# A hybrid decoder layer on one core: earlier table load and TensorE run-up, vectors behind x, and a reordered end

## The chip, the cores and the metric

The kernel runs on one core of a Trainium2 chip. The metric is the device time of one launch in microseconds. The kernel before took 1624.99 us (median of three runs, 1622.81 to 1625.93).

Five engines appear in the profile. TensorE is shown as PE for the matmuls and PEld for the loads of their stationary operand. VectorE is DVE, ScalarE is ACT, GpSimd is POOL, and SyncE is SP. SP issues nearly all transfers. ACT issues a few on a queue of its own, between its own instructions. Each engine works through its instructions in the order in which they stand.

## The reference

One layer works on x of 256 positions by 2048 channels, in float32. In short:

```
h    = rmsnorm(x) * norm_mix_w
proj = h @ w_in            -> q, k, v, z, b, a, p_in, g_a, g_b
q, k, v = silu(causal convolution over 4 positions); q and k normalised per head
o    = gated delta rule over 16 heads, chunked (a triangular solve per chunk)
y_a  = rmsnorm(o) * silu(z)
y_b  = (trailing means of p_in over 2, 4, 8, 16 positions - p_in) @ pool_w * pool_scale
x    = x + (sigmoid(g_a) * y_a + sigmoid(g_b) * y_b) @ w_out
h    = rmsnorm(x) * norm_ffn_w
gate, up = split(h @ w_up)
x    = x + (gelu(convolution over 3 positions of gate) * up) @ w_down
out  = rmsnorm(x) * norm_final_w
```

## The kernel before

The 256 positions are two tiles `t` of 128. All weights are streamed once in tiles of 256 rows by 512 columns (512 KB). There are 530 such transfers, two of them in another shape for the columns of b and a. A float32 product is formed from three fast products. `whi` is the weight rounded to the fast format (ACT, L110), `wlo` is the rest (DVE, L117), and the activations are split in the same way into `xhi` (ACT, L236) and `xlo` (DVE, L237). The matmuls of one weight tile are then twelve: L147 (`xhi` by `whi`), L148 (`xlo` by `whi`) and L149 (`xhi` by `wlo`), for two row blocks and two `t`. (The up projection swaps the roles of weights and activations, L171 and L172.) The weights go through three pools: `raw` with four buffers, `whi` and `wlo` with three each. `begin(n)` starts the load and the split of the next weights, `weights()` hands out the next pair.

The order of the instructions of each engine is not the order of the code. A scheduler places them by a simulated time line and by priority, engine by engine. The compiled order of an engine is therefore looked up, not read from the code.

At the start, x arrives as four tiles of 512 columns by `t` (`x_0` to `x_3`, L216), with the weight loads in between (L108). PE turns each x tile by transposes (L232) into `psg`. ACT makes `xhi` from it, scaled by the norm's weights `nmw`, which come in as rows (`nmrows`, L212) and are transposed as well (L223). DVE then makes `xlo`. The first product, the first 512 columns of k, runs over eight weight tiles. The small vectors of the layer (`vrows`, `cqrows`, `cfrows`, `alb`, `dtb`, `gwb`, and `psb`, which is pool_scale repeated on 128 partitions, 256 KB) come on ACT's queue. The squares of x for the norm (L310) run on ACT. Their sum gives `rs1`, which is first needed where the first product is taken out of the accumulator (L431).

In the middle, groups of four heads run their delta rule on DVE, POOL and small matmuls beside the big products. The up projection and the down projection follow.

At the end, the down projection adds 22 weight row blocks into four column accumulators `c` for each `t`. `acc[0]` and `acc[1]` lie in `psg`, `acc[2]` and `acc[3]` in `psm`. The last row block is taken in the order of `t`. Then for each `t` the accumulator is added to x (DVE, L848), squared and summed (ACT, L850), the four sums are reduced and scaled (DVE, L852 and L853), and raised to the power -1/2 (POOL, L854). Columns 2 and 3 are multiplied by the norm's weights `nfin` ahead of that (DVE, L857) and by the row factor after it (ACT, L864). Columns 0 and 1 get both at once (DVE, L861). Eight transfers write the result (SP, L865).

Of the kernel before, what the change touches and what calls it, by code (L numbers as in the profile page):

```python
# [20 lines left out]
EPS = 1e-6  # L21
# [4 lines left out]
B0 = 32  # L26
NR = P // B0
AHEAD = 2
WAIT = 5


@with_exitstack
def kernel(
# [44 lines left out]
    srcs = []  # L78
# [15 lines left out]
    made = []  # L94
    taken = [0]

    def weights():

        begin(taken[0] + AHEAD + 1)
        taken[0] += 1  # L100
        return made[taken[0] - 1]

    def begin(n):
        while len(made) < min(len(srcs), n):
            src = srcs[len(made)]
# [4 lines left out]
            nc.scalar.copy(hi, raw)  # L110
            if shape[1] == 8:
                lo = None
                nc.vector.tensor_tensor(hi[:, :, 32:64], raw[:, :, 0:32], hi[:, :, 0:32].bitcast(F32),
                                        op=ALU.subtract)
            else:
                lo = wpool.tile(shape, F32R, tag="wlo", name=nm("wlo"))
                nc.vector.tensor_tensor(lo, raw, hi.bitcast(F32), op=ALU.subtract)  # L117
            made.append((hi, lo))

# [16 lines left out]
    def gemm_a(lh, ll, nk):  # L136

        ps = pm()
        for c in range(nk // 2):
            if c == 1:  # L140
                while later:
                    later.pop(0)()
            hi, lo = weights()
            for kk in range(2):
                k = 2 * c + kk
                for t in range(2):
                    mm(ps[:, t, :], lh(k, t), hi[:, kk, :], start=(k == 0), stop=False)  # L147
                    mm(ps[:, t, :], ll(k, t), hi[:, kk, :], start=False, stop=False)  # L148
                    mm(ps[:, t, :], lh(k, t), lo[:, kk, :], start=False, stop=(k == nk - 1))  # L149
                side()  # L150
        return ps
# [45 lines left out]
    ones = cpool.tile([P, P], F32, name="ones")  # L197
# [28 lines left out]
    xhi, xlo = xhl[:, :, 0, :], xhl[:, :, 1, :]  # L226
    for k2 in range(KD // 2):
        pt = pg([P, 2, S])
        for kk in range(2):
            k = 2 * k2 + kk  # L230
            for t in range(2):
                nc.tensor.transpose(pt[:, kk, t * P : (t + 1) * P], x0[k // 4][:, t, (k % 4) * P : (k % 4 + 1) * P],  # L232
                                    ident)
        for kk in range(2):
            k = 2 * k2 + kk
            nc.scalar.activation(xhi[:, k, :], pt[:, kk, :], AF.Copy, scale=nmw[:, k : k + 1])  # L236
            nc.vector.scalar_tensor_tensor(xlo[:, k, :], pt[:, kk, :], nmw[:, k : k + 1], xhi[:, k, :].bitcast(F32),  # L237
                                           op0=ALU.mult, op1=ALU.subtract)

# [5 lines left out]

    ps_k0 = gemm_a(xh, xl, KD)


    NV = 16 + KF
    V_FFN, V_CB = 0, 16  # L250
# [15 lines left out]
    pv = pg()  # L266
# [3 lines left out]
    pv = pg()  # L270
# [4 lines left out]
    pv = pg()  # L275
# [88 lines left out]
    for c in range(2):  # L364
        hi, lo = weights()
        for kk in range(8):
            k = 8 * c + kk
# [86 lines left out]
    def gdn(g, kq, vT, res):  # L454
# [84 lines left out]
        yield  # L539
        for _ in range(WAIT):  # L540
            yield
# [16 lines left out]
        for h in range(4):  # L558
# [110 lines left out]
    for g in range(4):  # L669
# [88 lines left out]
    fp = ctx.enter_context(tc.tile_pool(name="ffn", bufs=1))  # L758
    xt = fp.tile([P, 2, D], F32, name="xt")
# [4 lines left out]
    for c in range(4):  # L764
        ps = gemm_a(at(mhi), at(mlo), KD)
        xs = xt[:, :, c * 512 : (c + 1) * 512]
        nc.vector.tensor_tensor(xs, xs, ps, op=ALU.add)
        for t in range(2):
            jk = cpool.tile([P, 512], F32, tag="sqj", name=nm("sqj"))
            nc.scalar.activation(jk, xs[:, t, :], AF.Square, accum_out=ssq4[:, t, c : c + 1])  # L770
        for k2 in range(2):
            pt = pg([P, 2, S])
            for kk in range(2):
                k = 4 * c + 2 * k2 + kk
                for t in range(2):
                    nc.tensor.transpose(pt[:, kk, t * P : (t + 1) * P], xt[:, t, k * P : (k + 1) * P], ident)
            for kk in range(2):
                k = 4 * c + 2 * k2 + kk
# [3 lines left out]
                                               op0=ALU.mult, op1=ALU.subtract)  # L782
# [45 lines left out]
    def down_part(kp, c, t, hi, lo):  # L828
        for kk in range(2):
            k = 2 * kp + kk  # L830
            mm(acc[c][t], lh(k, t), hi[:, kk, :], start=(k == 0), stop=False)  # L831
            mm(acc[c][t], ll(k, t), hi[:, kk, :], start=False, stop=False)  # L832
            mm(acc[c][t], lh(k, t), lo[:, kk, :], start=False, stop=(k == KF - 1))  # L833
# [6 lines left out]
                down_part(kp, c, t, *w)  # L840
    ws = [weights() for c in range(3)]
    ssq5 = cpool.tile([P, 2, 4], F32, name="ssq5")
    for t in range(2):
        for c in range(1, 4):
            down_part(LAST, c, t, *ws[c - 1])
        for c in range(4):
            xs = xt[:, t, c * 512 : (c + 1) * 512]
            nc.vector.tensor_tensor(xs, xs, acc[c][t], op=ALU.add)  # L848
            jk = cpool.tile([P, 512], F32, tag="sqj", name=nm("sqj"))
            nc.scalar.activation(jk, xs, AF.Square, accum_out=ssq5[:, t, c : c + 1])  # L850
        rs = cpool.tile([P, 1], F32, name=nm("rs"))
        nc.vector.tensor_reduce(rs, ssq5[:, t, :], axis=mybir.AxisListType.X, op=ALU.add)  # L852
        nc.vector.tensor_scalar(rs, rs, 1.0 / D, EPS, op0=ALU.mult, op1=ALU.add)  # L853
        nc.gpsimd.tensor_tensor(rs, rs, epsx[:, 0:1], op=ALU.pow)  # L854
        for c in (2, 3):
            xs = xt[:, t, c * 512 : (c + 1) * 512]
            nc.vector.tensor_tensor(xs, xs, nfin[:, c * 512 : (c + 1) * 512], op=ALU.mult)  # L857
        for c in (0, 2, 1, 3):
            xs = xt[:, t, c * 512 : (c + 1) * 512]
            if c < 2:  # L860
                nc.vector.scalar_tensor_tensor(xs, xs, rs, nfin[:, c * 512 : (c + 1) * 512],  # L861
                                               op0=ALU.mult, op1=ALU.mult)
            else:
                nc.scalar.activation(xs, xs, AF.Copy, scale=rs)  # L864
            nc.sync.dma_start(out[0, t * P : (t + 1) * P, c * 512 : (c + 1) * 512], xs)  # L865


# [29 lines left out]
```

## Time and profile before

| | |
|---|---|
| median of three runs | 1624.99 us (1622.81 to 1625.93) |
| the profiled execution: time, span | 1624.68 us, 1623.0 us |
| PE busy | 1577.3 us, 97% of the span |
| DVE, ACT, POOL busy | 1090.8, 753.5, 165.3 us |
| read from memory | 287.07 MB, 179 GB/s over the span |
| first matmul of a weight tile | 9.26 us after the span's start |
| last matmul ends | 1612.5 us after the span's start |

The span runs from the first instruction to the last; the profiled execution took 1.7 us more than its span. Times in the profile are counted from the span's start. A row of the time line has the start, the duration, the engine, the line of the kernel, the operation, what it writes and reads, and in brackets the idle time of the engine ahead of it and what ended it. Neighbouring equal instructions are merged into one row with their count; successive instructions overlap a little, so the durations of a group's members add up to more than its step. Matmuls are pipelined: the step from one start to the next, not the duration, is what a matmul costs in a stream.

### The profile page before, as it was taken

The numbers are of one execution on the slowest core, as the hardware profiler recorded it, in microseconds if no ns is written. First come the engines' busy times: TensorE is split into PE (matmuls) and PEld (weight loads), VectorE is DVE, ScalarE is ACT, GpSimd is POOL, SyncE is SP. The second block draws the span as 40 slices with busy tenths as digits, with TensorE's granted clock in tenths as the row PEclk, the third lists the DMA queues.
The fourth block names the chain that finished last, engine by engine and source line by source line (L and its number), as shares of the span: only waits on it lengthen the run. The fifth ranks groups of instructions, "written<-read, shape, count | busy, mean of one in ns | idle before, by whom it ended". The sixth has DMA issues, their size and how long they took to land.

```text
span 1623.0 us, 21418 instructions
## 1 busy us (share of the span) xinstructions
PE 1577.3 (97%) x8084; PEld 1319.9 (81%) x8084; DVE 1090.8 (67%) x1612; ACT 753.5 (46%) x977; POOL 165.3 (10%) x176
## 2 busy tenths in 40 slices
PE   8998999989999999989999999999999999999997
PEld 6876888878887788867788888888888888888886
DVE  5878757786678857796555766666667676444445
ACT  6454445434455435443355544444444444433334
POOL 1022100221013300141000000000000000000000
PEclk9999999999999999999999999999999999999999
DMA  7654645555556655555365655655655556655553
GB/s 247 182 164 150 195 145 177 169 171 173 156 156 171 174 173 164 168 147 170 138 228 181 187 190 186 191 185 192 192 185 192 185 193 204 200 194 194 194 194 131
DMA packets 159790, 291.62 MB, mean 180 GB/s; under 512 B 17974, under 2 KB 21062, under 8 KB 159302
## 3 DMA queue, kind: packets, MB, share of 16 engines
q1 hardware_dynamic: 157792, 285.77, 56.7%
q10 hardware_dynamic: 1894, 4.48, 0.8%
q8 instruction: 63, 1.03, 0.2%
q14 instruction: 41, 0.34, 0.1%
HBM read 287.07 MB, written 3.15 MB: 179 GB/s over the span
## 4 chain that ended last, share of the span: by engine, by line
PE 85%; DVE 7%; DMA 3%; issue 2%; POOL 2%; SPq 0%; DVEq 0%; POOLq 0%; ACT 0%
PE psm L149 12%; PE psm L148 11%; PE psm L147 11%; PE psm L171 10%; PE psg L171 10%; PE psg L172 5%; PE psm L172 5%; DVE wlo L117 3%; PE psg L831 2%; PE psg L832 2%; PE psg L833 2%; PE psm L831 2%; PE psm L833 2%; PE psm L832 2%; DVE tb L549 2%
## 5 line engine op out<-in xcount | busy, mean ns | idle before, releaser
L117 DVE TENSOR_TENSOR wlo<-raw,whi 128x1024 fp32r<-128x1024 f32 x528 | 658.6, 1249 | 416.8 <-ACT whi L110 406.3
L110 ACT CAST whi<-raw 128x1024 fp32r<-128x1024 f32 x530 | 557.5, 1053 | 769.5 <-PE psm L148 353.1
L149 PE MATMUL psm<-wlo,xhl 128*128 128x512 f32 x896 | 358.0, 400 | 18.3 <-DVE wlo L117 18.2
L147 PE MATMUL psm<-whi,xhl 128*128 128x512 f32 x896 | 355.6, 397 | 1.4 <-ACT xhl L236 1.4
L148 PE MATMUL psm<-whi,xhl 128*128 128x512 f32 x896 | 355.1, 396 | 0.0
L171 PE MATMUL psm<-fhl,whi 128*128 128x512 f32 x704 | 245.9, 396 | 0.0
L171 PE MATMUL psg<-fhl,whi 128*128 128x512 f32 x704 | 237.8, 394 | 0.0
L149 PEld LDWEIGHTS psm<-wlo,xhl 128*128 128x128 f32 x896 | 170.6, 190 | 58.3 <-DVE wlo L117 23.7
L147 PEld LDWEIGHTS psm<-whi,xhl 128*128 128x128 f32 x896 | 170.9, 191 | 35.8 <-ACT xhl L236 1.8
L148 PEld LDWEIGHTS psm<-whi,xhl 128*128 128x128 f32 x896 | 170.5, 190 | 35.4
L172 PE MATMUL psm<-fhl,wlo 128*128 128x256 f32 x704 | 194.2, 279 | 0.0
L172 PE MATMUL psg<-fhl,wlo 128*128 128x256 f32 x704 | 178.6, 279 | 0.0
L171 PEld LDWEIGHTS psm<-fhl,whi 128*128 128x128 f32 x704 | 131.4, 188 | 30.4
L171 PEld LDWEIGHTS psg<-fhl,whi 128*128 128x128 f32 x704 | 129.2, 188 | 24.0
L172 PEld LDWEIGHTS psg<-fhl,wlo 128*128 128x128 f32 x704 | 132.5, 188 | 6.9
L172 PEld LDWEIGHTS psm<-fhl,wlo 128*128 128x128 f32 x704 | 132.5, 188 | 1.1
L806 POOL TENSOR_TENSOR y<-y,rb 128x1024 f32<-128x1024 f32 x11 | 27.3, 2485 | 457.6 <-ACT y L805 457.6
L831 PE MATMUL psg<-whi,hhi 128*128 128x512 f32 x176 | 68.6, 390 | 0.0
L832 PE MATMUL psg<-whi,hlo 128*128 128x512 f32 x176 | 68.5, 389 | 0.0
L831 PE MATMUL psm<-whi,hhi 128*128 128x512 f32 x176 | 68.5, 389 | 0.0
L832 PE MATMUL psm<-whi,hlo 128*128 128x512 f32 x176 | 68.5, 389 | 0.0
L833 PE MATMUL psm<-wlo,hhi 128*128 128x512 f32 x176 | 68.5, 389 | 0.0
(232 smaller groups left out, 1617.7 us busy)
## 6 DMA issues: line engine op xcount, KB each, us to landing
raw<-in_w_in_dram SPq DMA_DIRECT2D x226, 512.0 KB, 3.8
raw<-in_w_up_dram SPq DMA_DIRECT2D x176, 512.0 KB, 3.5
raw<-in_w_down_dram SPq DMA_DIRECT2D x88, 512.0 KB, 4.3
raw<-in_w_out_dram SPq DMA_DIRECT2D x32, 512.0 KB, 3.6
raw<-in_pool_w_dram SPq DMA_DIRECT2D x8, 512.0 KB, 4.1
x<-in_x_dram SPq DMA_DIRECT2D x4, 512.0 KB, 8.0
lb<-cdd SPq DMA_DIRECT2D x16, 128.0 KB, 2.8
xt<-in_x_dram ACTq DMA_DIRECT2D x1, 2048.0 KB, 9.9
```

Of the source, the lines that this page charges most:

```text
L110: nc.scalar.copy(hi, raw)
L117: nc.vector.tensor_tensor(lo, raw, hi.bitcast(F32), op=ALU.subtract)
L147: mm(ps[:, t, :], lh(k, t), hi[:, kk, :], start=(k == 0), stop=False)
L148: mm(ps[:, t, :], ll(k, t), hi[:, kk, :], start=False, stop=False)
L149: mm(ps[:, t, :], lh(k, t), lo[:, kk, :], start=False, stop=(k == nk - 1))
L171: mm(ps[f], hi[:, kk, fs], rhl(k), start=(k == 0), stop=False, skip_group_check=True)
L172: mm(ps[f][:, 1, :], lo[:, kk, fs], rhl(k)[:, 0, :], start=False, stop=(k == nk - 1), skip_group_check=True)
L549: nc.vector.tensor_tensor(tb[:, :, j + 1 :], tb[:, :, j + 1 :], tv, op=ALU.subtract)
L806: nc.gpsimd.tensor_tensor(y, y, rb2b, op=ALU.mult)
L831: mm(acc[c][t], lh(k, t), hi[:, kk, :], start=(k == 0), stop=False)
L832: mm(acc[c][t], ll(k, t), hi[:, kk, :], start=False, stop=False)
L833: mm(acc[c][t], lh(k, t), lo[:, kk, :], start=False, stop=(k == KF - 1))
```

## The change

At the start, one element is copied on ACT ahead of all other work there, which puts the load of the function table at that place. Eleven matmuls of a tile of ones with itself are put ahead of PE's other work; their result is not used. The first x tile comes in two halves of 256 columns, with the first weight tile between them. The block of code that loads the small vectors, and the squares of x, are told to stand behind the last `xhi` on ACT. The load of `psb` is in a function that this block defines, and which is called further down.

At the end, the very last weight tile (column 3 of the last row block) gets buffers of its own, `whe` and `wle`, in a pool that the up projection has left. The additions, squares and the factor of each `t` have a higher priority in the scheduler. The sum of squares is split: three columns are summed first (`part`), the fourth is added in the scaling. For `t` = 0 all four columns are scaled in one step on DVE; for `t` = 1 two are, as before, and two are multiplied on DVE and scaled on ACT.

```diff
+RUNUP = 11
@@ begin(n)
-            hi = wpool.tile(shape, F32R, tag="whi", name=nm("whi"))
+            end = len(made) == len(srcs) - 1
+            hi = fp.tile(shape, F32R, tag="gs", bufs=2, name=nm("whe")) if end else \
+                wpool.tile(shape, F32R, tag="whi", name=nm("whi"))
...
+                lo = fp.tile(shape, F32R, tag="gs", bufs=2, name=nm("wle")) if end else \
+                    wpool.tile(shape, F32R, tag="wlo", name=nm("wlo"))
@@ start
+    first = cpool.tile([P, 1], F32, name="first")
+    nc.scalar.copy(first, ones[:, 0:1])
+    pv = pg()
+    for n in range(RUNUP):
+        mm(pv[:, :P], ones, ones, start=True, stop=True)
...
-        nc.sync.dma_start(xc, x[0, :, c * 512 : (c + 1) * 512].rearrange("(t p) d -> p t d", p=P))
         x0.append(xc)
-        begin(2 * c + 2)
+        n = 2 if c == 0 else 1
+        for h in range(n):
+            ds = slice(h * (512 // n), (h + 1) * (512 // n))
+            nc.sync.dma_start(xc[:, :, ds], x[0, :, c * 512 + ds.start : c * 512 + ds.stop]
+                              .rearrange("(t p) d -> p t d", p=P))
+            begin(2 * c + (2 if n == 1 else h + 1))
...
+            last_x = nc.scalar.activation(xhi[:, k, :], pt[:, kk, :], AF.Copy, scale=nmw[:, k : k + 1]).ins
...
+    rest = ExitStack()
+    rest.enter_context(tc.issue_after(last_x))
...
+    rest.close()
@@ end
+    def settle(t, c):
+        nc.vector.tensor_tensor(xs(t, c), xs(t, c), acc[c][t], op=ALU.add)
+        jk = cpool.tile([P, 512], F32, tag="sqj", name=nm("sqj"))
+        nc.scalar.activation(jk, xs(t, c), AF.Square, accum_out=ssq5[:, t, c : c + 1])
...
+        with tc.high_priority(offset=600):
+            for c in range(4):
+                settle(t, c)
+            part = cpool.tile([P, 1], F32, name=nm("part"))
+            nc.vector.tensor_reduce(part, ssq5[:, t, 0:3], axis=mybir.AxisListType.X, op=ALU.add)
+            nc.vector.tensor_scalar(part, part, 1.0 / D, EPS, op0=ALU.mult, op1=ALU.add)
+            rs = cpool.tile([P, 1], F32, name=nm("rs"))
+            nc.vector.tensor_scalar(rs, ssq5[:, t, 3:4], 1.0 / D, part, op0=ALU.mult, op1=ALU.add)
+            nc.gpsimd.tensor_tensor(rs, rs, epsx[:, 0:1], op=ALU.pow)
+        mine = (0, 1) if t else (0, 1, 2, 3)
         for c in (2, 3):
-            nc.vector.tensor_tensor(xs, xs, nfin[:, c * 512 : (c + 1) * 512], op=ALU.mult)
+            if c not in mine:
+                nc.vector.tensor_tensor(xs(t, c), xs(t, c), gains(c), op=ALU.mult)
         for c in (0, 2, 1, 3):
-            if c < 2:
+            if c in mine:
...
```

The compiled order shows what this moves. On PE at the start of the program, before (`whi_87` and `wlo_89` are the two parts of the first weight tile, `x_0` and `x_1` the first x tiles):

```order
L223 MATMUL psg_140<-ident,nmrows 128x16
L232 MATMUL psg_144<-ident,x_0_83 128x128 x4
L232 MATMUL psg_153<-ident,x_0_83 128x128 x4
L147 MATMUL psm_216<-whi_87,xhl 128x512
L232 MATMUL psg_162<-ident,x_1_97 128x128 x4
L232 MATMUL psg_171<-ident,x_1_97 128x128 x4
L148 MATMUL psm_216<-whi_87,xhl 128x512
```

PE at the same place in the changed kernel (`whi_101` is the first weight tile, `whi_108` the second; L213 is the run-up, L246 the transposes, L151 to L153 the former L147 to L149; the twelve matmuls of the first tile are cut here after two):

```order
L213 MATMUL psg_80<-ones 128x128 x11
L237 MATMUL psg_155<-ident,nmrows 128x16
L246 MATMUL psg_159<-ident,x_0_97 128x128 x4
L246 MATMUL psg_168<-ident,x_0_97 128x128 x4
L151 MATMUL psm_231<-whi_101,xhl 128x512
L152 MATMUL psm_231<-whi_101,xhl 128x512
...
L152 MATMUL psm_231<-whi_108,xhl 128x512
L246 MATMUL psg_177<-ident,x_1_112 128x128 x4
```

The transposes of `x_1` have moved from behind the first matmul to behind the fourteenth, and the run-up stands ahead of all.

On ACT at the start, before:

```order
L212 DMA nmrows<-in_norm_mix_w_dram 16x128
L253 DMA vrows<-in_norm_ffn_w_dram 16x128
L253 DMA vrows<-in_conv_ffn_b_dram 44x128
L255 DMA cqrows<-in_conv_qkv_w_dram 96x2x128
L258 DMA cfrows<-in_conv_ffn_w_dram 66x2x128
L110 ACT_TABLE_LOAD
L110 CAST whi_87<-raw_85 128x1024
L236 ACTIVATE xhl<-psg_144,nmw 128x256
```

ACT at the start of the changed kernel:

```order
L222 DMA nmrows<-in_norm_mix_w_dram 16x128
L210 ACT_TABLE_LOAD
L210 COPY first<-ones 128x1
L299 DMA psb_992<-in_pool_scale_dram 128x512
L113 CAST whi_101<-raw_99 128x1024
L250 ACTIVATE xhl<-psg_159,nmw 128x256
L250 ACTIVATE xhl<-psg_168,nmw 128x256
```

The table load stands right behind the first transfer, and five small transfers have left the place ahead of the first cast; the 256 KB transfer of `psb`, which stood behind the second cast, has come to stand ahead of the first.

On DVE at the end of the program, before, from the addition of column 2 of `t` = 1 (the two `psm` tiles are columns 2 and 3; `rs_13439` is the factor of `t` = 0, `rs_13483` that of `t` = 1):

```order
L848 TENSOR_TENSOR xt<-xt,psm_11870 128x512
L852 TENSOR_REDUCE rs_13439<-ssq_13408 128x1
L857 TENSOR_TENSOR xt<-xt,nfin 128x512
L853 TENSOR_SCALAR rs_13439<-rs_13439 128x1
L848 TENSOR_TENSOR xt<-xt,psm_11871 128x512
L861 SCALAR_TENSOR_TENSOR xt<-xt,rs_13439,nfin 128x512 x2
L857 TENSOR_TENSOR xt<-xt,nfin 128x512
L852 TENSOR_REDUCE rs_13483<-ssq_13408 128x1
L857 TENSOR_TENSOR xt<-xt,nfin 128x512
L853 TENSOR_SCALAR rs_13483<-rs_13483 128x1
L861 SCALAR_TENSOR_TENSOR xt<-xt,rs_13483,nfin 128x512 x2
```

DVE at the end of the changed kernel (L869 is the addition, L880 to L883 the sum of squares, L888 the multiplication by `nfin`, L891 the scaling; `rs_13457` is the factor of `t` = 0, `rs_13501` that of `t` = 1):

```order
L880 TENSOR_REDUCE part_13454<-ssq_13423 128x1
L881 TENSOR_SCALAR part_13454<-part_13454 128x1
L869 TENSOR_TENSOR xt<-xt,psm_11886 128x512
L883 TENSOR_SCALAR rs_13457<-ssq_13423,part_13454 128x1
L869 TENSOR_TENSOR xt<-xt,psm_11885 128x512
L891 SCALAR_TENSOR_TENSOR xt<-xt,rs_13457,nfin 128x512 x4
L880 TENSOR_REDUCE part_13498<-ssq_13423 128x1
L888 TENSOR_TENSOR xt<-xt,nfin 128x512 x2
L881 TENSOR_SCALAR part_13498<-part_13498 128x1
L883 TENSOR_SCALAR rs_13501<-ssq_13423,part_13498 128x1
L891 SCALAR_TENSOR_TENSOR xt<-xt,rs_13501,nfin 128x512 x2
```

The additions have moved ahead; behind the last of them stand four scalings of `t` = 0 in place of two, and both multiplications of `t` = 1 stand between its reduction and the next step of its factor.

More of the change, by code (lines that the diff above doesn't have):

```diff
@@ L115, in begin @@
             else:
-                lo = wpool.tile(shape, F32R, tag="wlo", name=nm("wlo"))
+                lo = fp.tile(shape, F32R, tag="gs", bufs=2, name=nm("wle")) if end else \
+                    wpool.tile(shape, F32R, tag="wlo", name=nm("wlo"))
                 nc.vector.tensor_tensor(lo, raw, hi.bitcast(F32), op=ALU.subtract)
@@ L235 @@
             k = 2 * k2 + kk
-            nc.scalar.activation(xhi[:, k, :], pt[:, kk, :], AF.Copy, scale=nmw[:, k : k + 1])
+            last_x = nc.scalar.activation(xhi[:, k, :], pt[:, kk, :], AF.Copy, scale=nmw[:, k : k + 1]).ins
             nc.vector.scalar_tensor_tensor(xlo[:, k, :], pt[:, kk, :], nmw[:, k : k + 1], xhi[:, k, :].bitcast(F32),
@@ L842, with xs, gains @@
     ssq5 = cpool.tile([P, 2, 4], F32, name="ssq5")
+    def xs(t, c):
+        return xt[:, t, c * 512 : (c + 1) * 512]
+    def gains(c):
+        return nfin[:, c * 512 : (c + 1) * 512]
+    def settle(t, c):
+        nc.vector.tensor_tensor(xs(t, c), xs(t, c), acc[c][t], op=ALU.add)
+        jk = cpool.tile([P, 512], F32, tag="sqj", name=nm("sqj"))
+        nc.scalar.activation(jk, xs(t, c), AF.Square, accum_out=ssq5[:, t, c : c + 1])
     for t in range(2):
@@ L845 @@
             down_part(LAST, c, t, *ws[c - 1])
[L846 to L853, printed above, removed]
@@ L854 @@
-        nc.gpsimd.tensor_tensor(rs, rs, epsx[:, 0:1], op=ALU.pow)
+        with tc.high_priority(offset=600):
[7 more added lines that the diff above has]
+            nc.gpsimd.tensor_tensor(rs, rs, epsx[:, 0:1], op=ALU.pow)
@@ L855 @@
+        mine = (0, 1) if t else (0, 1, 2, 3)
         for c in (2, 3):
-            xs = xt[:, t, c * 512 : (c + 1) * 512]
-            nc.vector.tensor_tensor(xs, xs, nfin[:, c * 512 : (c + 1) * 512], op=ALU.mult)
+            if c not in mine:
+                nc.vector.tensor_tensor(xs(t, c), xs(t, c), gains(c), op=ALU.mult)
         for c in (0, 2, 1, 3):
-            xs = xt[:, t, c * 512 : (c + 1) * 512]
-            if c < 2:
-                nc.vector.scalar_tensor_tensor(xs, xs, rs, nfin[:, c * 512 : (c + 1) * 512],
-                                               op0=ALU.mult, op1=ALU.mult)
-            else:
-                nc.scalar.activation(xs, xs, AF.Copy, scale=rs)
@@ L865 @@
-            nc.sync.dma_start(out[0, t * P : (t + 1) * P, c * 512 : (c + 1) * 512], xs)
+            if c in mine:
+                nc.vector.scalar_tensor_tensor(xs(t, c), xs(t, c), rs, gains(c), op0=ALU.mult, op1=ALU.mult)
+            else:
+                nc.scalar.activation(xs(t, c), xs(t, c), AF.Copy, scale=rs)
+            nc.sync.dma_start(out[0, t * P : (t + 1) * P, c * 512 : (c + 1) * 512], xs(t, c))
 _INS = ["x", "norm_mix_w", "w_in", "conv_qkv_w", "a_log", "dt_bias", "gdn_norm_w", "pool_w", "pool_scale",
```

## The prediction

> **What bounds the kernel now.** I read the page's busy times first, then the chain of work that ended last, then what PE waited for, and last the time line of the first 15 and the last 15 us, where the change lies.
>
> ```profile
> PE 1577.3 (97%) x8084; PEld 1319.9 (81%) x8084; DVE 1090.8 (67%) x1612; ACT 753.5 (46%) x977; POOL 165.3 (10%) x176
> PE 85%; DVE 7%; DMA 3%; issue 2%; POOL 2%; SPq 0%; DVEq 0%; POOLq 0%; ACT 0%
> PE psm L149 <- DVE wlo L117: 20.6, 14, 5.1
> ```
>
> PE is busy for 97% of the span and carries 85% of the chain. Its largest wait, 20.6 us for `wlo`, falls in the middle, where the work itself stays as it is. So the change can act through two numbers: how early PE comes into an unbroken stream, and how long the chain behind its last matmul is. First the start, PE and then the engines that feed it (bracketed: idle time and what ended it):
>
> ```profile
> 5.93 1.97 PE L232 MATMUL psg<-ident,x 128*128 128x128 f32 x8 [1.14 <-DMA x<-in_x_dram]
> 9.26 0.80 PE L147 MATMUL psm<-whi,xhl 128*128 128x512 f32 x1 [1.36 <-ACT xhl L236]
> 10.82 1.97 PE L232 MATMUL psg<-ident,x 128*128 128x128 f32 x8 [0.76 <-DMA x<-in_x_dram]
> ...
> 14.07 0.43 PE psm L148
> 15.13 0.23 PE psm L148
> ...
> 6.25 1.28 ACT L110 ACT_TABLE_LOAD   x1 [6.25 <-DMA x<-in_x_dram]
> 7.79 1.04 ACT L110 CAST whi<-raw 128x1024 fp32r<-128x1024 f32 x1 [0.25 <-DMA raw<-in_w_in_dram]
> 8.86 1.23 DVE L117 TENSOR_TENSOR wlo<-raw,whi 128x1024 fp32r<-128x1024 f32 x1 [3.67 <-ACT whi L110]
> 10.01 0.87 DVE L237 SCALAR_TENSOR_TENSOR xhl<-psg,nmw,xhl 128x256 fp32r<-128x256 f32 x2
> ```
>
> PE is unbroken from 10.82 us on, when `x_1` lands. The two short rows are from the chain, with the step of one matmul: 0.43 us up to 14.5, 0.23 from about 14.7. PE thus runs the first 3.9 us of its stream at half speed and loses 1.96 by it.
>
> **The start, part by part.** Table load: it ends at 7.53, and ACT still waits 0.25 us for the first weight tile. Earlier it saves nothing by itself, since that landing covers it; it would cost only with weights in before 7.53.
>
> Halves of x and vectors behind x: the price is when the first weight tile lands, now behind 256 KB of x in place of 512. The rate there (columns: window, its length, PE, PEld, DVE, ACT, POOL busy, clock, transfer share, GB/s):
>
> ```profile
> 2.00:4.00 2.00, 0.00 (x0) 0.00 (x0) 0.75 (x3) 0.00 (x0) 1.85 (x6) 1.00 0.69 180
> 4.00:6.00 2.00, 0.33 (x2) 0.25 (x3) 0.37 (x2) 0.00 (x0) 0.44 (x2) 1.00 0.88 228
> 6.00:8.00 2.00, 1.89 (x8) 1.49 (x8) 0.00 (x0) 1.50 (x2) 0.00 (x0) 1.00 0.98 347
> 8.00:10.00 2.00, 0.74 (x1) 0.29 (x1) 1.14 (x1) 2.00 (x4) 0.00 (x0) 1.00 1.07 398
> psb<-in_pool_scale_dram ACTq DMA_DIRECT2D x1, 256.0 KB
> cqrows<-in_conv_qkv_w_dram ACTq DMA_DIRECT2D x1, 96.0 KB, 7.2
> ```
>
> By 7.79 the queues had moved 0.36 + 0.46 + 1.79 x 0.347 = 1.44 MB, 0.39 more than `x_0` and the tile need. Behind a half x the tile needs 0.79 + 0.39 = 1.18 MB, reached at 7.0; but `psb`, 0.26 MB, now stands ahead of ACT's first cast and shares the engines. All of it ahead would make 1.44 MB, 7.75, so nothing won. The vectors that left that stretch give little back: their largest, 96 KB, landed 7.2 us after its issue at 2.5, so most of it came later than 7.8. I take the middle, 7.35, a gain of 0.4 (0 to 0.8), since `psb` is issued only behind the table load.
>
> From that cast at time c the rows give: `wlo` at c + 1.07, first `xlo` from c + 2.22, done 0.44 later, L148 at c + 2.7. That is 10.05, and `x_1`'s transposes no longer stand ahead of it: PE's stream starts 0.8 us earlier (0.3 to 1.1) with the same work left. `x_1` lands near 10.8 and is needed after 13 more matmuls, at least 3 us later.
>
> Run-up: eleven products, two passes each. A pass costs 0.11 us at full speed (four below in 0.61, the last of them 0.27 long) and at most the 0.25 of a slow transpose (eight in 1.97): 2.4 to 5.4 us from about 1.05, while x is on its way. Its price on the path is nil: it ends by 6.5, the four transposes behind it by 7.7, and `xhi` isn't asked for before the cast ends at 8.4.
>
> ```profile
> 209.65 0.61 PE L624 MATMUL psg<-vt,TT 128*128 128x128 f32 x4
> ```
>
> What it may bring is the clock. The same view in windows of 3.41 us, each ending where the clock did change:
>
> ```profile
> 141.03:144.45 3.42, 1.58 (x10) 1.03 (x8) 3.28 (x6) 2.50 (x5) 2.38 (x4) 1.00 0.42 143
> 144.45:147.86 3.41, 0.96 (x3) 0.49 (x3) 3.24 (x8) 1.22 (x3) 1.09 (x1) 1.00 0.50 145
> 147.86:151.27 3.41, 2.25 (x5) 1.82 (x6) 3.31 (x7) 0.00 (x0) 1.30 (x1) 0.50 0.30 73
> 519.91:523.33 3.42, 1.42 (x6) 1.20 (x7) 3.32 (x7) 0.34 (x1) 0.62 (x1) 1.00 0.15 20
> 523.33:526.74 3.41, 3.41 (x10) 2.62 (x9) 3.38 (x6) 1.75 (x3) 1.49 (x3) 0.50 0.76 226
> 755.43:758.84 3.41, 1.72 (x22) 1.47 (x23) 2.72 (x2) 1.03 (x4) 1.63 (x1) 1.00 0.83 269
> 758.84:762.26 3.42, 3.42 (x10) 2.65 (x9) 0.59 (x1) 1.04 (x1) 0.00 (x0) 0.50 0.44 163
> ```
>
> PE busy 0.96, 1.42 and 1.72 us of 3.41 was followed by half clock; 1.58 once was not. Full clock came back only after a wholly busy window (2.25 didn't do). In the changed kernel the run-up and the transposes keep PE busy from 1.05 to about 7.7, which fills a window and warms PE at a time b between 4.5 and 7.9. The next window holds what is left at full speed, (7.7 - b)/2.26 us (0.25 for 0.11), four transposes of the second half from about 8.2 (0.45), one matmul near 9 (0.25), and the stream from 10.05. For b from 4.5 to 6.5 that is 1.2 to 1.45 us busy; only for b over 7.3 is it over 1.6. So PE probably falls back just as its stream begins. With this execution's phase it would be slow from 10.05 to 14.7, losing 2.3 us for 1.96. Stream 0.8 earlier less 0.4: the start gains 0.4 (-0.4 to 1.1; 2.8 if PE stays warm: 0.8 + 1.96).
>
> The Trainium skill (TensorE: Matmul & The Clock Gate, Part 1) says that half clock comes back only after at least one idle window of about 3.4 us. By that rule PE would stay warm, as no gap is that long, and the sum be 2.4 us lower. The trace differs: windows in which PE was busy for 0.96, 1.42 and 1.72 us were enough.
>
> Squares behind `xhi`: eight of 0.64 us leave ACT's early stretch. `rs1` comes at about 39 us in place of 24.7; its first reader stands on ACT at 38.7, and PE transposes that reader's result only at 67.3.
>
> ```profile
> 24.74 0.16 DVE L315 TENSOR_SCALAR rsh<-rs 128x2 f32<-128x2 f32 x1
> 38.73 1.25 ACT L431 ACTIVATE ev<-psm,rs 128x512 f32<-128x512 f32 x2
> L192 PE MATMUL psg<-ident,ev x24: 270/273/306, 67.3 to 117.4; 128*128 128x128 f32 x24
> ```
>
> So it costs nothing (cover: 28 us). In the middle the order moves by at most one weight tile; I set 0.
>
> **The end.** PE's last matmul ends at 1612.5 either way: `whe` has its tile by the landing that the old order had, and 3 us in hand. DVE and POOL behind it:
>
> ```profile
> 1613.23 1.41 DVE L861 SCALAR_TENSOR_TENSOR xt<-xt,rs,nfin 128x512 f32<-128x512 f32 x2
> 1614.56 0.68 DVE L857 TENSOR_TENSOR xt<-xt,nfin 128x512 f32<-128x512 f32 x1
> 1615.43 0.16 DVE L852 TENSOR_REDUCE rs<-ssq 128x1 f32<-128x4 f32 x1 [0.18 <-ACT sqj L850]
> 1615.50 0.68 DVE L857 TENSOR_TENSOR xt<-xt,nfin 128x512 f32<-128x512 f32 x1
> 1616.10 0.15 DVE L853 TENSOR_SCALAR rs<-rs 128x1 f32<-128x1 f32 x1
> 1616.33 0.55 POOL L854 TENSOR_TENSOR rs<-rs,epsx 128x1 f32<-128x1 f32 x1 [3.13 <-DVE rs L853]
> 1616.91 1.42 DVE L861 SCALAR_TENSOR_TENSOR xt<-xt,rs,nfin 128x512 f32<-128x512 f32 x2 [0.67 <-POOL rs L854]
> ```
>
> The new order puts four scalings of `t` = 0 where two stood, at 0.665 us each (1613.23 to 1614.56 for two): 1613.23 + 2.66 = 1615.89. The reduction takes 0.07, the two multiplications 0.60 each (1615.50 to 1616.10): 1617.16 for the next step. The split sum adds one dependent small step, 0.2: 1617.36. POOL 0.23 later, the last scalings 0.58 after that: 1618.17 for 1616.91. ACT's last square, 0.7 us earlier by the additions ahead of it, no longer ends a wait, since DVE comes to it late. What follows, four transfers, is the same. So the end costs 1.26 us (1.0 to 1.5).
>
> **Sum.** 1624.68 (the profiled execution; 0.3 under the median) - 0.4 + 1.26 = 1625.5; on the median 1625.8. What a measurement of this kernel tells from no change is about 0.2%, 3.25 us: 1621.7 to 1628.2.
>
> **Rivals.** *PE stays warm* (0.2): if a window of 1.5 us holds the clock, as one of 1.58 did: 1624.99 - 2.8 + 1.26 = 1623.5. Against it: 1.42 and 1.72 did not.
>
> *The small vectors slowed the start* (0.2): they may be why the queues moved 180 and 228 GB/s and not 398. At 398 from 2.0 us, 1.18 MB are there by 5.0, PE is unbroken from the run-up on and streams warm from 8.3. By 14.7 that is 6.4 us of the stream at full speed, where before 1.96 were done, so the gain is 4.4: 1624.99 - 4.4 + 1.26 = 1621.8 or less. Against it: few of their bytes lie in that stretch.
>
> *Slower, in the middle* (0.15): in the first group DVE's `sz` step of 1.2 us stands ahead of the transpose that POOL's `T` needs. If PE reaches L589 before `T` is ready, it waits as it did once, and half clock follows (the last windows above): 1.72 + 3.41/2 = 3.4, 1629.2.
>
> ```profile
> PE psg L589 <- POOL T L574: 1.7, 1, 1.7
> 183.13 1.21 DVE L730 SCALAR_TENSOR_TENSOR sz<-gate,psm 128x1024 f32<-128x1024 f32 x1
> ```
>
> It decides only if `T` comes more than one weight tile (2.7 us) late, since in the compiled order the twelve matmuls of one more weight tile stand ahead of L589 there.
>
> *The start does nothing* (0.1): `psb` takes the vectors' place in full: 1624.99 + 1.26 = 1626.3.
>
> **How the numbers follow.** The forecast has 0.35, its own range 1624.3 to 1627.3 (the three runs spread by 3.1). Over the cases 8 in 10 lie from 1620.8 to 1629.2. Faster by over 0.2%: most of the second rival and a little of the first, 0.24. Slower: the third, and the tails of two others, 0.18. The rest, 0.58, is within.
>
> **What would show it.** The start: the first cast at 7.0 to 7.8, L152 unbroken from about 10.05, with steps of 0.43 until 14 or later; steps of 0.23 from the first speak for the first rival, a cast near 5 for the second. The end: L891 four times from 0.76 us behind PE's last matmul, the last two 5.7 behind it (4.4 before). A wait of L607 (the former L589) speaks for the third. I am wrong if DVE's end is no longer than before, or if PE waits in the middle where it did not.

## The result and the profile after

The changed kernel takes 1625.40 us (median of 22 runs, 1621.80 to 1629.51), the kernel before 1624.24 us (22 runs, 1620.48 to 1626.87). The ratio is 1.0008 (95% interval 1.0002 to 1.0015), 1.3 us more (0.3 to 2.4). The profiled execution, 1628.51 us with a span of 1626.8, is 3.1 us over its own median, so not all of its parts are typical; the experiments show which of them repeat.

The page of the changed kernel and what its PE waited for:

```profile
PE 1583.1 (97%) x8106; PEld 1324.9 (81%) x8106; DVE 1092.5 (67%) x1614; ACT 753.7 (46%) x976; POOL 165.6 (10%) x176
PE 86%; DVE 7%; issue 3%; DMA 2%; POOL 1%; SPq 0%; ACT 0%; POOLq 0%; DVEq 0%
PE psm L153 <- DVE wlo L121: 21.6, 15, 5.1
```

PE bounds the kernel as before. The busy time has grown by 5.8 us, most of it the run-up (4.87 us on the time line), which lies in time that was idle.

The start on the time line:

```profile
1.28 1.28 ACT L210 ACT_TABLE_LOAD   x1 [1.28 <-PEq L910]
1.35 0.40 ACTq L299 DMA_DIRECT2D psb<-in_pool_scale_dram  x1
7.89 1.05 ACT L113 CAST whi<-raw 128x1024 fp32r<-128x1024 f32 x1 [5.12 <-DMA raw<-in_w_in_dram]
9.37 0.80 PE L151 MATMUL psm<-whi,xhl 128*128 128x512 f32 x1
10.65 0.79 PE L152 MATMUL psm<-whi,xhl 128*128 128x512 f32 x1 [0.49 <-DVE xhl L251]
```

The table is loaded 5 us earlier, and ACT then waits 5.12 us for the first weight tile, which comes at 7.89 as it came at 7.79 before. PE's stream is unbroken from 10.65 (10.82 before). The transfer of `psb` is issued at 1.35, while the table is being loaded. The same stretch in windows of 3.41 us that end where the clock changed (columns as in the prediction's windows):

```profile
2.17:5.58 3.41, 3.41 (x18) 3.41 (x18) 0.87 (x3) 0.59 (x2) 2.24 (x6) 1.00 0.85 251
5.58:9.00 3.42, 1.43 (x11) 1.04 (x11) 0.20 (x2) 1.10 (x2) 0.84 (x1) 1.00 1.02 367
9.00:12.41 3.41, 2.92 (x8) 1.85 (x7) 2.81 (x5) 2.57 (x5) 0.66 (x1) 0.50 1.04 387
12.41:15.82 3.41, 3.41 (x9) 2.64 (x9) 2.50 (x3) 1.05 (x2) 0.00 (x0) 0.50 1.05 390
```

In these views the clock column shows 1.00 also ahead of the first change on record; there the steps tell. Those of the run-up are 0.21 us in the first window, and 0.11 is the step of such a pass at the full clock. So the run-up fills the first window at half clock, and the clock is full from 5.58. In the next window PE is busy for 1.43 us only, and from 9.00 the clock is at half again, for two windows. The stream runs at half speed from 10.65 to 15.82.

The end, DVE and POOL behind the last addition:

```profile
1615.10 0.69 DVE L869 TENSOR_TENSOR xt<-xt,psm 128x512 f32<-128x512 f32 x1 [0.55 <-PE psm L851]
1615.71 2.73 DVE L891 SCALAR_TENSOR_TENSOR xt<-xt,rs,nfin 128x512 f32<-128x512 f32 x4
1618.36 0.15 DVE L880 TENSOR_REDUCE part<-ssq 128x1 f32<-128x3 f32 x1
1618.42 1.28 DVE L888 TENSOR_TENSOR xt<-xt,nfin 128x512 f32<-128x512 f32 x2
1619.81 0.21 DVE L883 TENSOR_SCALAR rs<-ssq,part 128x1 f32<-128x1 f32 x1
1620.10 0.55 POOL L884 TENSOR_TENSOR rs<-rs,epsx 128x1 f32<-128x1 f32 x1 [4.92 <-DVE rs L883]
1620.69 1.42 DVE L891 SCALAR_TENSOR_TENSOR xt<-xt,rs,nfin 128x512 f32<-128x512 f32 x2 [0.67 <-POOL rs L884]
```

The four scalings of `t` = 0 and the two multiplications stand between the last addition and the factor of `t` = 1. The last scalings start 5.59 us behind the start of the last addition; before they started 4.40 behind it (1612.51 to 1616.91).

Between start and end the profiled execution lost 2.1 us more against that of the kernel before: 3.2 us at one place, of which 1.3 came back further on, and 0.3 ahead of it. At that place DVE waits for `lb`, which comes back from memory, and the next `wlo` stands behind that wait. The row of the changed kernel, and then that of the kernel before:

```profile
501.40 0.42 DVE L565 TENSOR_TENSOR tmp<-lb,tb 128x248 f32<-128x248 f32 x1 [4.36 <-DMA lb<-cdd]
```

```profile
498.98 0.42 DVE L547 TENSOR_TENSOR tmp<-lb,tb 128x248 f32<-128x248 f32 x1 [2.68 <-DMA lb<-cdd]
```

PE then waited 1.42 us at 503.8, where it had not waited before. Another window at half clock stood at 534.65. That `lb` caused it isn't shown: PE waits for a `wlo` there in both kernels, 1.96 us (until 533.65) and 1.95 us (until 531.23 in the kernel before). In the changed kernel this wait falls into the one window of 3.41 us ahead of 534.65, in which PE is busy for 1.45 us; in the kernel before it lies across the edge of two windows, with 2.54 and 2.34 us. The order of the instructions is the same there in both kernels.

### The profile page after: what moved, and what is told of

It is laid out like the page before. It is cut to its first block, busy times and chain, and to the rows that moved or that the text cites. A ratio compares the mean times of both kernels' runs of the same rounds, so it can differ in the third digit from the quotient of the medians.

```text
span 1626.8 us, 21460 instructions
## 1 busy us (share of the span) xinstructions
PE 1583.1 (97%) x8106; PEld 1324.9 (81%) x8106; DVE 1092.5 (67%) x1614; ACT 753.7 (46%) x976; POOL 165.6 (10%) x176
## 4 chain that ended last, share of the span: by engine, by line
PE 86%; DVE 7%; issue 3%; DMA 2%; POOL 1%; SPq 0%; ACT 0%; POOLq 0%; DVEq 0%
PE psm L153 12%; PE psm L152 12%; PE psm L151 12%; PE psm L175 10%; PE psg L175 10%; PE psg L176 5%; PE psm L176 5%; DVE wlo L121 3%; PE psg L849 2%; PE psg L850 2%; PE psg L851 2%; PE psm L849 2%; PE psm L850 2%; PE psm L851 2%; DVE tb L567 2%
## 5 line engine op out<-in xcount | busy, mean ns | idle before, releaser
L153 PE MATMUL psm<-wlo,xhl 128*128 128x512 f32 x896 | 358.3, 400 | 19.3 <-DVE wlo L121 19.3
L151 PE MATMUL psm<-whi,xhl 128*128 128x512 f32 x896 | 356.6, 398 | 0.0
L153 PEld LDWEIGHTS psm<-wlo,xhl 128*128 128x128 f32 x896 | 171.3, 191 | 59.3 <-DVE wlo L121 24.5
L151 PEld LDWEIGHTS psm<-whi,xhl 128*128 128x128 f32 x896 | 171.6, 191 | 34.6 <-ACT xhl L250 0.3
```

## The experiments

Besides the time, two numbers are read from each profile: when the first weight tile's cast starts, and how far the last scalings lie behind the start of the last addition.

**The end alone.** The kernel before with the diff's parts on `begin` and on the end.

> The kernel before with the end of the change alone (additions and squares ahead, split sum, four scalings of t = 0 on DVE, last weights in their own buffers). Theory A, the end is a fixed cost: the last scalings start 5.6 us behind PE's last matmul where 4.4 stood before, and the time is 1.2 us over the kernel before (0.8 to 1.6). Rival B, the end is covered by the output transfers, which are the same eight: time within 0.3 us of before although the scalings start later. Both expect the start and the middle as before, to 0.1 us up to the eighth weight tile.

Measured: 1626.27 us, ratio 1.0004 (0.9995 to 1.0013), which tells nothing by itself. The time line of its end:

```profile
1614.50 0.69 DVE L854 TENSOR_TENSOR xt<-xt,psm 128x512 f32<-128x512 f32 x1 [0.55 <-PE psm L836]
1620.09 1.41 DVE L876 SCALAR_TENSOR_TENSOR xt<-xt,rs,nfin 128x512 f32<-128x512 f32 x2 [0.67 <-POOL rs L869]
```

The distance is 5.59 us, to the hundredth that of the changed kernel. The span ends 6.2 us behind the last scalings, as before (6.1), so the output transfers cover nothing, and rival B falls. The eighth weight tile was cast 0.6 us later than before (29.39 against 28.80), and PE waited near 503 us here too. So start and middle were not as before to 0.1 us, as both theories had expected; they vary from execution to execution.

**The start alone.** The changed kernel with the end of the kernel before.

> The changed kernel with the old end, so the start of the change alone. Theory A, the start only moves where the cold window of PE's clock falls: first weight tile cast at 7.8 to 7.9 as before, PE's stream from about 10.65, time within 0.7 us of before on the median. Rival C, the start or the order it leaves in the middle is what costs: the changed kernel's profile lay 2.1 us further behind after 503 us, so the time would be 2 to 3 us over before and the same place near 503 us would show it again.

Measured: 1624.14 us, ratio 0.9989 (0.9979 to 0.9999). So the start costs nothing and gains somewhat, and rival C falls: this profile has no wait of PE near 503 us at all. The cast came at 7.27, the stream at 10.02, and the clock was full again at 13.21. Theory A isn't met to the letter either: it had the cast at 7.8 and the stream at 10.65, and the ratio puts the gain at 1.8 us (0.2 to 3.4), where it allowed 0.7.

**The scalings of t = 0 shared again.**

```diff
-        mine = (0, 1) if t else (0, 1, 2, 3)
+        mine = (0, 1)
```

> The changed kernel with the scalings of t = 0 shared as before: two on DVE, two multiplied on DVE ahead and scaled on ACT. Theory A, the four scalings of t = 0 that stand ahead of the sum of t = 1 on DVE are the cost of the end: last scalings about 4.4 us behind PE's last matmul (5.6 in the changed kernel), time 1.2 us under the changed kernel. Rival D, the split sum and the multiplications behind it are the cost: still 5.3 us or more, and no gain over 0.3 us.

Measured: 1624.17 us, 1.2 us under the changed kernel by the medians and 1.8 by the ratios; against the kernel before 0.9997 (0.9986 to 1.0008). Its end:

```profile
1610.93 0.68 DVE L869 TENSOR_TENSOR xt<-xt,psm 128x512 f32<-128x512 f32 x1
1615.53 1.42 DVE L891 SCALAR_TENSOR_TENSOR xt<-xt,rs,nfin 128x512 f32<-128x512 f32 x2 [0.45 <-POOL rs L884]
```

4.60 us: one line gives 1.0 of the 1.19 us back, and rival D falls. Of the rest, POOL's step for `t` = 1 carries a part: it took 0.93 us here, beside a multiplication on DVE, and 0.55 in the changed kernel. DVE waited 4.62 us for `lb` in this execution (498.48), with the same order as in the changed kernel and in the one above, where it was 2.91.

**The last weights in the common buffers.** The parts of the diff on `whe` and `wle` undone. In the changed kernel the own buffers let PE take column 3 ahead of column 2, so that the column added last belongs to `part`.

> The changed kernel with the last weight tile in the common buffers again. In the changed kernel its own buffers let column 3 go ahead of column 2 on PE, so that column 2, which the partial sum needs, is the last to be added. Theory A, DVE's queue (four scalings, two multiplications) sets the end and not the order of the columns: column 3 is last again, and the last scalings still start 5.5 to 5.7 us behind the start of the last addition. Rival H, the split sum would have paid if column 3 had stayed last: the last scalings start 4.9 us behind the last addition or earlier.

Its end on the time line:

```profile
1610.37 0.69 DVE L866 TENSOR_TENSOR xt<-xt,psm 128x512 f32<-128x512 f32 x1 [0.55 <-PE psm L848]
1615.95 1.42 DVE L888 SCALAR_TENSOR_TENSOR xt<-xt,rs,nfin 128x512 f32<-128x512 f32 x2 [0.67 <-POOL rs L881]
```

5.58 us, as theory A had it: with column 3 last the split sum still brings nothing, since DVE comes to it late. Measured were 1627.66 us, ratio 1.0022 (1.0012 to 1.0032). That the median is 2 us over the changed kernel stays open; the profile (1623.72 us, the fastest of its eight runs) shows no reason.

**A longer run-up.**

```diff
-RUNUP = 11
+RUNUP = 24
```

> The changed kernel with 24 run-up matmuls in place of 11, so that PE is busy without a gap from 1.05 us until the halves of x are transposed. Theory A, PE fell back to half clock at 9.0 us because the window from 5.6 to 9.0 was mostly idle: now the clock stays full from the first full window on, the stream runs with steps of 0.23 from its first matmul, and the ninth weight tile comes 2.6 us earlier than in the changed kernel; time 2.6 us lower, about 1622.8. Rival E, the longer run-up only delays the transposes of x and the clock falls back anyway: ninth weight tile within 0.5 us of the changed kernel or later.

Measured: 1624.25 us, ratio 0.9994 (0.9983 to 1.0004). The first full window and the two behind it, and then, from the time line, the wait in the second:

```profile
4.99:8.41 3.42, 3.42 (x32) 3.35 (x30) 0.00 (x0) 0.85 (x1) 0.87 (x1) 1.00 1.00 336
8.41:11.82 3.41, 2.30 (x20) 2.00 (x18) 2.67 (x4) 2.31 (x5) 0.64 (x1) 1.00 1.04 393
11.82:15.23 3.41, 3.41 (x15) 2.33 (x14) 3.31 (x7) 3.25 (x8) 0.00 (x0) 1.00 1.05 390
```

```profile
10.83 1.06 PE L246 MATMUL psg<-ident,x 128*128 128x128 f32 x8 [1.11 <-DMA x<-in_x_dram]
```

The clock stays full, as theory A said, and the ninth weight tile comes 1.2 us earlier (30.82 against 32.03), so rival E falls. But the scheduler put the transposes of `x_1` ahead of the first product again, and PE waited for `x_1` until 10.83. The thirteenth weight tile was cast at 40.57, 1.5 us ahead of the changed kernel (42.10) and not 2.6. The time can't be put down to the run-up alone: from about 35 us on until the last weight tiles this kernel has the order of the kernel before, not that of the changed kernel.

**No run-up.** `RUNUP = 0`.

> The changed kernel without the run-up matmuls (no matmul of ones with itself). Theory A, the eleven matmuls warm PE but the idle stretch behind them lets it go cold again, so they bring nothing that lasts: cold window of 3.4 to 6.8 us from the start of the stream at 10 to 10.9 us, as in the changed kernel (5.2 in its profile, 4.1 and 3.2 in two further ones with the same start), ninth weight tile within 0.8 us of the changed kernel, time within 1 us of it. Rival F, the run-up shortens the cold stretch: without it the stream stays cold until 16 us or later and the time is 1 us or more above.

Measured: 1617.42 us, ratio 0.9965 (0.9953 to 0.9977), by the two ratios 7 us under the changed kernel. Neither theory said that. In its profile the start gave 2.5 us of it (thirteenth tile at 39.62), though the last kernel below, with the same start, has 40.94. With no run-up ahead of them, the first half's transposes and `xhi` were done early, the stream ran from 8.44, and the window of its profile that ends where the clock came back is this one (half clock by its steps, 0.43 us up to 11.17, whatever the column shows):

```profile
7.85:11.26 3.41, 2.82 (x9) 2.34 (x10) 2.35 (x3) 2.43 (x4) 1.03 (x1) 1.00 1.05 398
```

The rest lies in the first group, which the edit doesn't touch; it is taken up below.

**psb behind x as well.**

```diff
 def scales(g):
+        late = ExitStack()
+        if g == 0:
+            late.enter_context(tc.issue_after(last_x))
         nc.scalar.dma_start(psb, ...)
+        late.close()
```

> The changed kernel with the 256 KB transfer of psb behind the last xhi as well. Theory A, psb shares the engines with the first weight tile: that tile's cast moves from 7.3 to 8.1 (the profiles so far with this start: 7.89, 7.27, 8.11, 7.56) to about 6.9 (256 KB at 0.39 MB per us are 0.65 us, half to all of it ahead of the tile), and PE's stream starts 0.3 to 0.8 us earlier; time 0.3 to 0.8 us lower. Rival G, the transfers of x and the weights that are queued on SP take the room: the cast stays at 7.3 or later.

Measured: 1618.72 us, ratio 0.9960 (0.9948 to 0.9972). The first cast:

```profile
6.92 1.04 ACT L113 CAST whi<-raw 128x1024 fp32r<-128x1024 f32 x1 [4.16 <-DMA raw<-in_w_in_dram]
```

The cast comes at 6.92, as theory A had it; in the eight profiles with this table load and `psb` ahead it came at 7.00 to 8.11. By the thirteenth tile the kernel is 1.1 us ahead of the kernel before (40.54 against 41.63). The remaining 5 us come later: from the 25th to the 67th cast it takes 134.1 us, without the run-up 132.3, the changed kernel 139.1, the kernel before 138.9. Here too the changed kernel's profile isn't typical: four others with its order there (the start alone, the scalings shared, the common buffers, and the other end below) took 136.5 to 137.3.

Those two kernels have one and the same order of all engines from the second hundred of PE's instructions to the end, and it is another one than in the changed kernel: the scheduler, which works through a simulated time line, has tipped over. Waits of PE in the first group, of the kernel before:

```profile
130.06 0.50 PE L149 MATMUL psm<-wlo,xhl 128*128 128x512 f32 x1 [0.86 <-DVE wlo L117]
145.23 0.50 PE L147 MATMUL psm<-whi,phi 128*128 128x512 f32 x1 [2.62 <-ACT phi L711]
149.02 0.80 PE L149 MATMUL psm<-wlo,xhl 128*128 128x512 f32 x1 [2.83 <-DVE wlo L117]
```

and without the run-up:

```profile
140.24 0.50 PE L152 MATMUL psm<-whi,plo 128*128 128x512 f32 x1 [0.56 <-DVE plo L730]
145.81 0.50 PE L153 MATMUL psm<-wlo,xhl 128*128 128x512 f32 x1 [2.33 <-DVE wlo L121]
```

6.3 us of waits have become 2.9, and the two windows of half clock behind them (3.4 us lost) are gone, which makes 6.8 us; 6.6 were measured. Over all profiles with each order the stretch takes 133.3 us in the mean (four, 132.3 to 134.1) against 137.2 in the changed kernel's order (five) and 139.0 in that of the kernel before (two), so the other order is worth about 4 to 6 us there.

**One part of that order alone.** In the other order ACT casts `phi` ahead of the gate. The kernel before with only that:

```diff
+            late.enter_context(tc.issue_after(first_phi[0]))
         tb = gate(ps, "th")
+        late.close()
```

> The kernel before with one order added in the middle, nothing at the start or the end: in the first group ACT's two tanh steps of the gate are told to stand behind the first phi cast. (The two kernels that came out 6 to 7 us faster, without the run-up and with psb late, both have phi ahead of the gate there; the kernel before and the changed one have it behind, and PE waits 2.6 us for phi.) Theory J, that place in the middle is where those two gained: PE's wait ahead of phi's first product falls from 2.6 us to under 1, less half clock follows, and the time is 3 to 6 us under before. Rival K, the earlier start of those two gained it by phase, or other moved instructions did: time within 1 us of before.

Measured: 1625.84 us, ratio 1.0010 (1.0001 to 1.0019). Theory J falls, as PE's two waits there show:

```profile
145.14 0.51 PE L147 MATMUL psm<-whi,phi 128*128 128x512 f32 x1 [1.54 <-ACT phi L712]
150.71 0.80 PE L148 MATMUL psm<-whi,plo 128*128 128x512 f32 x1 [5.07 <-DVE plo L715]
```

The wait for `phi` is 1.1 us shorter, but PE goes straight into the other products of `phi` then, and waits 5.07 us for `plo`, with less work to put between. So the gate's place alone doesn't gain; that it is the order of PE and DVE around it is likely but not shown, and which of the moved instructions carry the gain is open.

**Another end.** The partial sum takes columns 0, 1 and 3; columns 2 and 3 are scaled on DVE, 0 and 1 on ACT; one scaling of `t` = 0 stands behind the sum of `t` = 1.

```diff
-            for c in range(4):
-                settle(t, c)
+            for j, c in enumerate((0, 1, 3, 2)):
+                square = settle(t, c, j)
...
+            if t == 0 and c in (3, ):
+                behind.enter_context(tc.issue_after(factor))
+            if t == 0 and c in (0, 1):
+                behind.enter_context(tc.issue_after(square))
```

> The changed kernel with another end: the partial sum takes columns 0, 1 and 3, since column 2 is added last; columns 0 and 1 of both t are multiplied on DVE ahead and scaled on ACT, behind the last square; the second scaling of t = 0 on DVE stands behind the sum of t = 1. Theory A, DVE's queue behind the last addition sets the end: addition 0.6, multiplication 0.6, one scaling 0.67, reduction and two small steps 0.45, then 0.25 and 0.55 on POOL, so ACT's last scalings start 3.2 us behind the start of the last addition and DVE's 0.1 later (5.6 in the changed kernel, 4.4 before), and the time is 2.3 us under the changed kernel. Rival I, the output transfers, eight of which crowd together then, take the gain back: time within 0.5 us of the kernel before.

Measured: 1624.78 us, ratio 0.9999 (0.9990 to 1.0008). DVE and POOL at its end:

```profile
1613.60 0.68 DVE L869 TENSOR_TENSOR xt<-xt,psm 128x512 f32<-128x512 f32 x1
1616.04 0.74 DVE L897 SCALAR_TENSOR_TENSOR xt<-xt,rs,nfin 128x512 f32<-128x512 f32 x1
1616.20 0.99 POOL L885 TENSOR_TENSOR rs<-rs,epsx 128x1 f32<-128x1 f32 x1 [2.11 <-DVE rs L884]
1617.22 1.42 DVE L897 SCALAR_TENSOR_TENSOR xt<-xt,rs,nfin 128x512 f32<-128x512 f32 x2 [0.45 <-POOL rs L885]
```

3.62 us in place of 5.59, where 3.3 was expected: POOL's step took 0.99 us beside a scaling on DVE, and 0.55 wherever DVE stood idle. The span ends 6.5 us behind the last scalings and not 6.1, where the eight transfers are issued within 3.9 us (4.9 before). Of 1.97 us some 1.6 are left, and 0.4 against the kernel before. So the time is within 0.5 us of the kernel before, as rival I had it, though the transfers took back only 0.4 us of the gain.

**The parts together.** This end with psb late, and this end without the run-up.

> The changed kernel with psb behind the last xhi and with the end of the earlier experiment (partial sum of columns 0, 1 and 3, two scalings each on DVE and ACT, the sum of t = 1 ahead of the last scalings of t = 0). If the parts add up: 6.5 us under before from psb's run, 1.5 us more from the end, so about 1616.5 us, last scalings 3.6 us behind the last addition. If the end's gain is taken back by the transfers it is 1618.5.

> The changed kernel without the run-up matmuls and with the same new end. If the parts add up: 5.7 to 7 us under before from the run without the run-up, 1.5 us more from the end, so about 1616 us. If the run-up is worth something on the chip beyond what the order gives, it is slower than the kernel with psb late and the same end by 1 us or more.

Measured: with psb late 1615.62 us (1615.15 to 1615.79), ratio 0.9950 (0.9937 to 0.9963), which beats both kernels; without the run-up 1617.69 us, ratio 0.9965 (0.9953 to 0.9976). With psb late the parts add up, and a little more than forecast. Without the run-up the ratio is no better than with the old end, so the 1.5 us don't show there. The order of the middle is the same in both. They differ in `psb` and in the run-up, so how the 2 us between them divide is not shown. The first has the earlier cast, and here the run-up did hold the clock, which stayed full from 4.35 to 144.3 us; in the profile with psb late and the same start it did not (window 6.89 to 10.30, PE busy for 2.10 us, then half clock). The cast on its time line, and the two windows behind the change of the clock:

```profile
6.64 1.04 ACT L113 CAST whi<-raw 128x1024 fp32r<-128x1024 f32 x1 [3.87 <-DMA raw<-in_w_in_dram]
```

```profile
4.35:7.76 3.41, 2.11 (x17) 1.72 (x16) 0.33 (x3) 1.12 (x2) 0.28 (x1) 1.00 0.94 327
7.76:11.18 3.42, 2.57 (x14) 1.75 (x13) 3.40 (x5) 2.56 (x5) 0.00 (x0) 1.00 1.04 380
```

## Why the prediction was right

The forecast was 1625.8 us, the sum of a start that gains 0.4 and an end that costs 1.26. Measured are 1625.4. The steps one by one:

- *The table load saves nothing.* Right: ACT waited 5.12 us for weights behind it. (Four small transfers, not five, stood ahead of the first cast before.)
- *The first cast at 7.35.* A little early. Five executions with this start have 7.89, 7.27, 8.11, 7.00 and 7.96, mean 7.65; three with the old start 7.79, 7.93 and 7.97, mean 7.90. The gain is 0.25 and not 0.4. That `psb` takes the room was right: without it the cast came at 6.92 and 6.64. The reason for taking the middle was wrong: `psb` isn't issued behind the table load but at 1.35, right behind the first weight tile (1.28), and 7.65 is near the 7.75 that the prediction reckoned with all of `psb` ahead.
- *The stream 0.8 us earlier.* Too much. In the same executions it starts at 10.65, 10.02, 10.86, 9.76 and 10.72, mean 10.40, against 10.82, 11.19 and 10.95, mean 10.99: 0.6.
- *The clock falls back as the stream begins.* Right, in all five: windows with PE busy for 1.43, 1.51, 1.54, 1.73 and 1.90 us were followed by half clock, as was 2.10 us with psb late. From the stream's start to the full clock it takes 3.2 to 5.7 us, mean 4.5, with the run-up, and 3.9 to 5.1, mean 4.4, with the old start. Without a run-up, in the two kernels that leave it out, it took 2.8 and 3.8. So eleven run-up matmuls mostly bring nothing that lasts; the clock held behind eleven in one profile, that of the fastest kernel, whose cast comes earlier. The forecast took one execution's phase for it (4.65 us), which was luck of the right size.
- *The rule of the Trainium skill* (TensorE: Matmul & The Clock Gate, Part 1), that half clock needs an idle window, does not agree with these windows: PE was at work for 42% and more of each.
- *The start gains 0.4.* The thirteenth cast, against that of the kernel before as profiled, is at +0.47, -1.06, +0.23, -0.19 and +0.11 with the new start, mean -0.1, and at 0, +0.57 and +0.73 with the old one, mean +0.4. The gain is 0.5, with a scatter of about the same size, and the start alone runs at 0.9989.
- *The squares and vectors cost nothing.* PE's list of waits shows no new wait there.
- *The middle, set at 0.* The order did move by one weight tile, and L607 waited for `T` as before (1.9 us in all, 1.7 before), so the rival on the slower side did not come about. What the step left out is that single executions differ by 2 us and more there: DVE waited from 2.7 to 4.6 us for `lb`, and each wait of PE can cost a window of half clock. It also left out that the moved order may gain: from the 25th to the 67th cast four of its five profiles are about 2 us under the kernel before. Whether that holds on the median is not shown.
- *The end costs 1.26.* Measured 1.18 or 1.19 in six profiles with this end (one of them with common buffers), and 1.0 came back with one line undone. The prediction did not see that column 3 moves ahead of column 2; it made no difference, as the run with common buffers shows.
- *PE stays warm, and the vectors held up the start.* The first of these rivals happened in none of the five executions, but did with the longer run-up and in the fastest kernel. The second is refuted: even with `psb` gone the cast does not come near 5 us.

0.5 less and 1.2 more make 0.7; 1.3 were measured (0.3 to 2.4). The two halves measured alone (0.9989 and 1.0004) come to 0.9993, 2.4 us under the 1.0008 of both together, which is about as much as the three intervals allow, so the sum is not confirmed to better than that. That 1625.8 and 1625.4 lie only 0.4 apart is in part luck: the forecast added 0.8 to 1624.99, and the kernel before was measured at 1624.24 the second time.

## What to carry to other kernels

Work that is put ahead of a dependent step on an in-order engine costs most of its length at the end of a program (here 1.0 us for two scalings of 0.67 each), even where it saves work on another engine: count what stands between the last input and the last factor. Warming an engine up pays only if it stays busy until the real stream begins; look at the window behind the run-up, not at the run-up. Where a scheduler sets the order, an edit at one place can reorder another: compare the compiled order of the whole program and its waits, since here that was worth 4 to 6 us and the edits that were meant to gain were worth 1.

## What the runs showed of the hardware that was not expected

- POOL's power step on one column of 128 took 0.55 us while DVE stood idle or added from an accumulator, and 0.93 to 1.01 while DVE worked on two inputs from SBUF (the kernels with the other end, both times in each, and the one with the scalings shared again, once).
- How busy a window must be to hold the clock has no sharp bound here: 2.11 and 2.30 us of 3.41 held it, 1.90 and 2.10 did not, though 1.58 once did in the kernel before. To bring it back 2.82 us were enough without the run-up, while 2.92 were not in the changed kernel.
- DVE's wait for the small transfer `lb` near 500 us was 2.91 and 4.62 us in two profiles with the same order up to there; PE waited 0 and 1.68 us behind it.
